# Alternating the two row halves in 64-row products, and four kinds of steps that resume a set time later

## The chip, the cores and the metric

The kernel runs on one core of one Trainium2 chip. The metric is device time in microseconds (us), from launch to the end of the core's last instruction; less is better. TensorE (PE) multiplies 128x128 weight tiles with moving operands of up to 512 columns into PSUM, which has 8 banks of 512 float32 columns here. VectorE (DVE), ScalarE (ACT) and GpSimd (POOL) do the elementwise work, and SyncE (SP) issues most DMAs.

## The reference

Two models of two layers each, on 256 tokens of width 1024, one after the other, float32. The first alternates gated MLPs with a mixer of two attentions; the second has a mixer of three branches and a gated MLP with a short convolution.

```python
x = x + 0.5 * swiglu(rms_norm(x, g1), w_gate, w_up, w_down)       # d_ff 2816
x = x + hybrid_mixer(rms_norm(x, g), ...)     # NSA, 8 heads of 64; MoBA, 8 heads of 64
x = x + 0.5 * swiglu(rms_norm(x, g2), ...)
# second model
h = rmsnorm(x, norm1_g)
p_rw, p_ret, p_sg, gates = split(h @ w_in)
# RWKV-7, 8 heads of 64, a state step for each token:
state = state * w_t + (state @ -kk_t) x (kk_t * a_t) + v_t x k_t ;  y_t = state @ r_t
# retention, 4 heads: q, k of 64, v of 128, in chunks of 128 tokens:
scores = einsum('bhnid,bhnjd->bhnij', qc, kc) * decay_in ;  inner = scores @ vc
x = x + sum(sigmoid(gates) * (branches @ w_branch)) @ w_out
x = x + conv_ffn(rmsnorm(x, norm2_g))
```

MoBA has one block at this length, so it is causal attention. The RWKV-7 recurrence is computed in two chunks of 128 tokens: products over a head's 64 features between the decayed r, kk, k and b give 128x128 matrices; a strictly triangular system is solved in blocks of 32.

## The kernel before, in words

The 256 tokens are two tiles `t` of 128 rows. All large products are done in three passes of float32r: an operand is split into a rounded part and the rest (`wh`, `wl` of a weight tile; `xh`, `xl` of the transposed activations). A weight tile of 512 KB is loaded into `raw` on SP's queue (5 buffers), ACT casts it to `wh`, DVE subtracts to `wl`, and TensorE takes it with 24 matmuls of 256 columns (banks `cf`, `pj`) or 12 of 512 (`pj`, `acc`). That stream runs from start to end.

Everything else is cut into steps. A step is what a Python generator does between two `yield`s (`norm`, `rw_keys`, `rw_products`, `rw_chain`, `group_norm`, ...). `tick` (line 295), called between the matmuls of the stream, adds steps of tasks that are due, by rank. Due times come from a cost model of the builder (`Meter`, line 130): `step` (line 272) remembers the modelled end of the last instruction off TensorE in a step, and after a bare `yield` the task is due 0.1 us after that end. The model is only a plan: it fixes the order of the instructions on each engine, and the engines then run through it in order. All instructions are issued through one wrapper, so the trace shows line 191 for each; tiles tell them apart.

Names used below:

- `norm` (531): the transposed x; then the row factor `xr` by ACT (`junk`) and POOL, and, for `wide`, a step whose product `pt<-ident,xr` spreads it over partitions for `factor`. Eight phases have it, for two `t` each.
- `rw_keys` (1468): `pn` and POOL's power give `n` (one number for a token and a head), `pr` spreads it; then `pL`, the products of all 16 heads and tiles, copied to `Ld` and masked to `Lo`. `Ld` goes out to memory and back as `Lc`.
- `rw_chain` (1634): 31 rounds on DVE (`Tt`, `T`) invert the blocks from `Lc`; the result goes out and back to `dbd` by 9 DMAs, and the substitution (`pS`) reads that.
- `rw_products` (1598): for each `t` and head, `pM` (64 rows; one product of 128 columns, one of 256), copied under a mask to `mrb` and `lm`; in the next step `pX` and `pY` multiply `lm` with v.
- `group_norm` (1727): the branch output `Y`, then transposed (`pt<-ident,Y`).
- `moba` (970): scores `sc<-kmT,qmT`; `retention` (1288): scores `rs<-qkT`.

Head pairs are stacked: rows 0 to 63 of `kr`, `bh`, `KT`, `qkT`, `kmT`, `qmT` hold the even head, rows 64 to 127 the odd one. A float32 product counts as two matmul records in the trace, one of float32r as one.

Of the kernel before, what the change touches and what calls it, by code (L numbers as in the profile page):

```python
# [17 lines left out]
P = 128  # L18
# [204 lines left out]
class Builder:  # L223
# [48 lines left out]
    def step(self, task):  # L272
        self.meter.last = self.meter.t["PE"]
        try:
            y = next(task.gen)
        except StopIteration:
            self.tasks.remove(task)
            return
        if y is None:
            task.ready = self.meter.last + 0.1  # L280
        elif callable(y):
            task.cond = y
        else:
            task.ready = self.meter.of(y) + 0.1
# [246 lines left out]
    def norm(self, t, gi, wide=False, outer=None):  # L531


        nc = self.nc
        F = "p (k f) -> p k f"
        for i in range(2):
            yield from self.have(t, i)
            pt = self.ps("pt")
            for k in range(4):
                c = slice(k * P, (k + 1) * P)  # L540
                nc.tensor.transpose(pt[:, c], self.half(t, i)[:, c], self.ident)
            k = slice(i * 4, i * 4 + 4)
            g = self.gains if outer is None else self.both
            o = gi * KD if outer is None else 0
            g = g[:, o + i * 4:o + i * 4 + 4, None].to_broadcast([P, 4, P])
            xg = self.u("xg").rearrange(F, f=P)
            nc.vector.tensor_tensor(xg, pt.rearrange(F, f=P), g, ALU.mult)
            nc.scalar.copy(self.xh[:, k, t], xg)
            yield [self.xh[:, i * 4, t]]
            nc.vector.tensor_tensor(self.xl[:, k, t], xg, self.xh[:, k, t].bitcast(F32), ALU.subtract)  # L550
            self.ready_xT[t] = i + 1
        yield
        if outer is not None:
            ro = yield from self.row_norm(t, outer)
        r = yield from self.mean_sq(t)
        if outer is not None:
            nc.gpsimd.tensor_tensor(r, r, ro, ALU.mult)
        self.rstd[t] = r
        if wide:
            yield  # L560
            if not self.factor:
                self.factor.append(self.u("factor"))
            pt = self.ps("pt")
            nc.tensor.matmul(pt[:, :P], r.to_broadcast([P, P]), self.ident, start=True, stop=True)
            nc.scalar.copy(self.factor[0][:, t * P:(t + 1) * P], pt[:, :P])
            self.factored.append(t)
# [150 lines left out]
        self.nc.scalar.copy(o, pt)  # L717
        return o.rearrange("p (k f) -> p k f", f=P)

    def attend(self, jobs, place, factor, fresh):  # L720

# [1 line left out]
        nc = self.nc  # L725
        sms, pes, ptss = {}, {}, {}
        for i in range(len(jobs) + 4):
# [24 lines left out]
            if i < len(jobs):  # L752
                t, j, units = jobs[i]
                w = P * (t + 1)
                mask = self.c("cmask")[:, 256 - w:256]
                sms[i] = []
                for score, _ in units:
                    ps = self.ps("sc")
                    score(ps, w)
                    sm = self.u("sm")  # L760
                    mn = self.small("mn", 2, 6)
                    for e in range(2):
                        c = slice(e * w, (e + 1) * w)
                        nc.vector.tensor_tensor_reduce(sm[:, c], ps[:, c], mask, op0=ALU.add, op1=ALU.min, scale=-0.125,
                                                       scalar=BIG, accum_out=mn[:, e:e + 1])
                    sms[i].append((sm, mn))
# [27 lines left out]
    def mixer1(self, l, after):  # L794
# [75 lines left out]
        def vs(e, kb, g):  # L870
            return kv1[kb][:, 384 + g * 64:448 + g * 64] if e == 0 else kv2[kb][:, 128 + g * 64:192 + g * 64]
# [25 lines left out]
        def nsa():  # L897
# [26 lines left out]

            def unit(t, h):
                g = h // 4

                def score(ps, w):
                    q = qst[t, g][:, h % 4]
                    nc.tensor.matmul(ps[:, :2 * w], q, kh[g][:, :, 0:t + 1], start=True, stop=False)  # L930
                    nc.tensor.matmul(ps[:, :2 * w], q, kl[g][:, :, 0:t + 1], start=False, stop=True)

                return score, lambda e, kb: vs(e, kb, g)

            def factor(t, j, r, sums):
                nc.vector.reciprocal(r, sums)
# [7 lines left out]
            def place(t, j, u, e):  # L944
                return out_of(t)[64 * u:64 * u + 64, j * P:(j + 1) * P]

            for y in self.attend(jobs, place, factor, False):
                yield y
                n += 1
                if n in (1, 2):  # L950
                    for z in cmp:
                        yield z
                        break
                if n == 3:
                    yield from cmp
                for t, at in ((0, 8), (1, 12)):
                    if n == at:
                        self.begin(split_oT(0, t, out[t]), 0)
# [11 lines left out]
        def moba():  # L970
# [10 lines left out]
                return out[t][64 * u:64 * u + 64, (2 * j + e) * P:(2 * j + e + 1) * P]  # L981

            def unit(t, j, u):
                def score(ps, w):
                    b = slice(64 * u, 64 * u + 64)
                    for e in range(2):
                        for kb in range(t + 1):
                            nc.tensor.matmul(ps[:, e * w + kb * P:e * w + (kb + 1) * P], qmT[t][b, 2 * j + e],
                                             kmT[kb][b, 2 * j + e], start=True, stop=True)

                return score, lambda e, kb: vm[kb][:, (4 * j + 2 * e + u) * 64:(4 * j + 2 * e + u + 1) * 64]

            def factor(t, j, r, sums):
                nc.vector.reciprocal(r, sums)

            n = 0
            for y in self.attend([(t, j, [unit(t, j, u) for u in range(2)]) for t in range(NT) for j in range(2)],
                                 place, factor, True):
                yield y
                n += 1  # L1000
                for t, at in ((0, 6), (1, 8)):
                    if n == at:
                        self.begin(split_oT(1, t, out[t]), 0)
# [284 lines left out]
    def retention(self, qk, rv, rg, done):  # L1288
# [23 lines left out]
        yield  # L1312
        for t in range(NT):
            sc = self.u("rsc")
            for par in range(2):
                b = 64 * par
                ps = self.ps("rs")
                for j in range(2):
                    nc.tensor.matmul(ps[:, j * P:(j + 1) * P], qkT[t][b:b + 64, 2 + j], qkT[t][b:b + 64, j],
                                     start=True, stop=True)  # L1320
                nc.vector.tensor_tensor(sc.rearrange("p (j r f) -> p j r f", j=2, r=2)[:, :, par],
                                        ps[:, :256].rearrange(F, f=P),
                                        self.c("rdec").rearrange("p (j r f) -> p j r f", j=2, r=2)[:, :, par], ALU.mult)
            yield
            y = self.u("yret")
# [142 lines left out]
    def rw_keys(self, l, st):  # L1468
# [16 lines left out]
        n = self.small("n2", 16, 2)  # L1485
        nc.vector.tensor_scalar_max(n, pn[:, :16], 1e-24)
        nc.gpsimd.tensor_tensor(n, n, self.mh, ALU.pow)
        yield
        for q in range(2):
            pr = self.ps("pr")  # L1490
            kk.append(self.pairs("kk"))
# [30 lines left out]
            off[t, par] = self.u("Lo").rearrange(F, f=P)  # L1522
            tt(off[t, par], pv, self.c("moff")[:, None].to_broadcast([P, 4, P]), ALU.mult)

        late = None
        for t in range(NT):
            for par in range(2):
                b = 64 * par
                pL = self.ps("pL")
                for j in range(4):  # L1530
                    mm(pL[:, j * P:(j + 1) * P], BT[j // 2][b:b + 64, j % 2, t], kr[j // 2][b:b + 64, j % 2, t, 0],
                       start=True, stop=True)
                s0 = (t * 2 + par) * 4
                pv = pL.rearrange(F, f=P)
                for blk in range(4):
                    c = slice(32 * blk, 32 * blk + 32)
                    nc.scalar.copy(Ld[c, s0:s0 + 4], pv[c, :, c])
                if late:
                    rest(*late)
                late = t, par, pv  # L1540
                yield
        rest(*late)
        for blk in range(4):
            nc.sync.dma_start(sysd[blk].rearrange("y s t -> s y t"), Ld[32 * blk:32 * blk + 32])
        Lc = self.up.tile([P, 32, 32], F32, tag="kr", name="Lc")
# [52 lines left out]
    def rw_products(self, l, st):  # L1598
# [13 lines left out]
        for t in range(NT):  # L1612
            m = mrb[t]
            pX, pY = self.ps("pX", "pq"), self.ps("pY", "pq")
            for h in range(8):
                b, q, e = 64 * (h % 2), h // 4, h // 2 % 2
                pM = self.ps("pM")
                mm(pM[:, 0:P], BT[q][b:b + 64, e, t], kr[q][b:b + 64, e, t, 1], start=True, stop=True)
                mm(pM[:, P:3 * P], KT[q][b:b + 64, e, t], kr[q][b:b + 64, e, t].rearrange("p z f -> p (z f)"), start=True, stop=True)
                lm = st["lm"][h % 4]  # L1620
                nc.vector.copy_predicated(m[:, h], mk[:, 0:P], pM[:, 0:P])
                nc.vector.copy_predicated(lm, mk[:, P:3 * P], pM[:, P:3 * P])
                yield
                c = slice(h * 64, (h + 1) * 64)
                self.narrow(pX[:, c], lm[:, 0:P], v[t][:, c])
                self.narrow(pY[:, c], lm[:, P:2 * P], v[t][:, c])
            X.append(self.u("X"))
            Y.append(self.u("Y"))
            nc.scalar.copy(X[t], pX)
# [97 lines left out]
    def group_norm(self, lnx, y, v, bonus, g, done):  # L1727
# [18 lines left out]
        tt(y, y, lnx[0], ALU.mult)  # L1746
        tt(y, y, bv, ALU.add)
        tt(y, y, g, ALU.mult)
        yield
        yield from done(y)  # L1750


# [95 lines left out]
```

## Time and profile before

| | |
|---|---|
| three runs, median | 2075.59 us (2074.72 to 2077.48) |
| profiled execution | 2073.28 us, its span 2071.3 us |
| TensorE matmul busy | 2013.7 us, 97% |
| DVE, ACT, POOL busy | 67%, 50%, 7% |
| DMA | 343.98 MB, 166 GB/s on average |
| granted TensorE clock, mean | 0.990 |

A busy TensorE is the time in which at least one matmul record is open. Records overlap, since matmuls are pipelined, so the distance from one start to the next is the time that one costs. The granted clock is 1.00 at 2.4 GHz and 0.50 at 1.2 GHz.

### The profile page before, as it was taken

Reading aid. Unit: us, or ns where it says so; the run is one execution under the profiler, and the core shown is the slowest. Engines: PE = TensorE matmul, PEld = TensorE weight load, DVE = VectorE, ACT = ScalarE, POOL = GpSimd, SP = SyncE. Lnnn points to the kernel's source line nnn. Section 1 sums busy time; section 2 is a strip of 40 time slices with the busy share of each in tenths; the row PEclk is TensorE's granted clock in tenths of the full one; section 3 lists DMA queues with packets and bytes.
Section 4 is the critical chain, followed back from the end, with each engine's and each line's share of the span. In section 5 each row is a group of like instructions: output and inputs, shape, how many; then the busy total and the mean of one; then the engine's idle time right before and its main releaser. Section 6 shows DMA issues by size and latency. Waiting matters only on the chain. (4 is left out here: it accounts for less than half of the span.)

```text
span 2071.3 us, 33930 instructions
## 1 busy us (share of the span) xinstructions
PE 2013.7 (97%) x13548; PEld 1776.8 (86%) x13548; DVE 1394.7 (67%) x2101; ACT 1043.6 (50%) x1605; POOL 149.8 (7%) x168
## 2 busy tenths in 40 slices
PE   8999999999999999999999999999999999999998
PEld 8998878998999887799887777889988877789997
DVE  6665666664666467666567957669955886667983
ACT  5444675443444366544455434456636444446652
POOL 0000000000000010000021031210001003110000
PEclk9999999999999999999999999999999999999999
DMA  9655623656655562356653434555664453465562
GB/s 315 195 181 152 213 83 113 198 177 194 218 180 185 157 214 92 122 174 193 186 175 114 147 112 136 180 162 177 191 200 134 133 153 98 153 192 176 177 194 97
DMA packets 246733, 343.98 MB, mean 166 GB/s; under 512 B 22064, under 2 KB 182192, under 8 KB 246448
## 3 DMA queue, kind: packets, MB, share of 16 engines
q1 hardware_dynamic: 244224, 340.20, 52.8%
q8 instruction: 106, 1.74, 0.4%
q10 hardware_dynamic: 2352, 1.63, 0.3%
q14 instruction: 51, 0.42, 0.1%
HBM read 339.68 MB, written 2.10 MB: 165 GB/s over the span
## 5 line engine op out<-in xcount | busy, mean ns | idle before, releaser
L191 DVE TENSOR_TENSOR wl<-raw,wh 128x1024 fp32r<-128x1024 f32 (+1 forms) x614 | 750.8, 1236 | 323.9 <-ACT wh L191 323.0
L191 ACT CAST wh<-raw 128x1024 fp32r<-128x1024 f32 (+1 forms) x614 | 639.3, 1046 | 585.9 <-PE cf L191 179.6
L191 PE MATMUL cf<-xh,wh 128*128 128x256 f32 x2112 | 524.7, 285 | 2.4 <-ACT wh L191 2.4
L191 PE MATMUL cf<-xl,wh 128*128 128x256 f32 x2112 | 523.0, 285 | 0.0
L191 PEld LDWEIGHTS cf<-xh,wh 128*128 128x128 f32 x2112 | 409.3, 194 | 3.0 <-ACT wh L191 2.8
L191 PEld LDWEIGHTS cf<-xl,wh 128*128 128x128 f32 x2112 | 409.2, 194 | 0.2
L191 PE MATMUL cf<-xh,wl 128*128 128x256 f32 x2112 | 300.3, 285 | 0.0
L191 PEld LDWEIGHTS cf<-xh,wl 128*128 128x128 f32 x2112 | 275.3, 194 | 0.0
L191 PE MATMUL pj<-wh,xh 128*128 128x512 f32 (+1 forms) x544 | 223.0, 410 | 4.5 <-DVE gate L191 2.0
L191 PE MATMUL pj<-wl,xh 128*128 128x512 f32 (+1 forms) x544 | 211.1, 388 | 0.0
L191 PE MATMUL pj<-wh,xl 128*128 128x512 f32 (+1 forms) x544 | 210.4, 387 | 0.0
L191 PE MATMUL acc<-wh,h 128*128 128x512 f32 x528 | 207.0, 392 | 0.0
L191 PE MATMUL acc<-wh,hl 128*128 128x512 f32 x528 | 205.6, 389 | 0.0
L191 PE MATMUL acc<-wl,h 128*128 128x512 f32 x528 | 205.5, 389 | 0.0
L191 PEld LDWEIGHTS pj<-wh,xh 128*128 128x128 f32 x544 | 102.8, 189 | 36.7 <-issue 9.9
L191 DVE TENSOR_TENSOR up<-cf,factor 128x512 f32<-128x512 f32 x132 | 90.6, 688 | 56.3 <-PE cf L191 56.2
L191 PEld LDWEIGHTS pj<-wh,xl 128*128 128x128 f32 x544 | 102.8, 189 | 21.4
L191 PEld LDWEIGHTS pj<-wl,xh 128*128 128x128 f32 x544 | 103.1, 189 | 16.9 <-DVE wl L191 0.9
L191 PEld LDWEIGHTS acc<-wh,hl 128*128 128x128 f32 x528 | 99.1, 188 | 20.9
L191 PEld LDWEIGHTS acc<-wh,h 128*128 128x128 f32 x528 | 99.2, 188 | 20.0
L191 PEld LDWEIGHTS acc<-wl,h 128*128 128x128 f32 x528 | 99.2, 188 | 19.9
L191 POOL TENSOR_SCALAR xv<-ss 128x1 f32<-128x1 f32 x24 | 20.2, 840 | 1142.6 <-ACT junk L191 1142.6
(314 smaller groups left out, 2489.6 us busy)
## 6 DMA issues: line engine op xcount, KB each, us to landing
raw<-w_in SPq DMA_DIRECT2D x156, 512.0 KB, 4.3
raw<-w_ffn_gate SPq DMA_DIRECT2D x88, 512.0 KB, 4.4
raw<-w_ffn_up SPq DMA_DIRECT2D x88, 512.0 KB, 4.8
raw<-w_ffn_down SPq DMA_DIRECT2D x88, 512.0 KB, 4.2
raw<-ffn_w_up SPq DMA_DIRECT2D x88, 512.0 KB, 4.7
raw<-ffn_w_down SPq DMA_DIRECT2D x44, 512.0 KB, 4.5
raw<-w_out SPq DMA_DIRECT2D x32, 512.0 KB, 3.7
raw<-w_branch SPq DMA_DIRECT2D x24, 512.0 KB, 4.5
```

What stands on the lines that cost most here:

```text
L191: return f(*args, **kw)
```

## The change

A `yield` of a number makes a task due that many modelled microseconds after the step's last instruction off TensorE. Four steps use it: the spreading of `xr` (5.0), of `n` (3.0), the products `pX`, `pY` (0.8), and the transposing of `Y` (2.0). The products over 64 rows of two heads, of the even and of the odd rows, are written alternately, into two PSUM banks that are claimed first. So `rw_products` takes two heads in a step and `pL` both row halves of a token tile. In `attend` a job's two score banks are claimed before its products; the NSA scores, which have 128 rows, keep their order.

```diff
@@ step
+        elif isinstance(y, float):
+            task.ready = self.meter.last + y
@@ norm
-            yield
+            yield 5.0
@@ attend
-                for score, _ in units:
-                    ps = self.ps("sc")
-                    score(ps, w)
+                banks = [self.ps("sc") for _ in units]
+                scores([x for x, _ in units], banks, w)
+                for ps in banks:
@@ moba
-                    for e in range(2):
-                        for kb in range(t + 1):
+            def scores(keys, banks, w):
+                for e in range(2):
+                    for kb in range(keys[0][0] + 1):
+                        for (t, j, b), ps in zip(keys, banks):
                             nc.tensor.matmul(ps[:, e * w + kb * P:e * w + (kb + 1) * P], qmT[t][b, 2 * j + e],
                                              kmT[kb][b, 2 * j + e], start=True, stop=True)
@@ retention
+            rs = [self.ps("rs") for par in range(2)]
+            for j in range(2):
+                for par in range(2):
+                    b = slice(64 * par, 64 * par + 64)
+                    nc.tensor.matmul(rs[par][:, j * P:(j + 1) * P], qkT[t][b, 2 + j], qkT[t][b, j], start=True, stop=True)
...
@@ rw_keys
-        yield
+        yield 3.0
...
-            for par in range(2):
-                b = 64 * par
-                pL = self.ps("pL")
-                for j in range(4):
...
+            pL = [self.ps("pL") for par in range(2)]
+            for j in range(4):
+                for par in range(2):
+                    b = slice(64 * par, 64 * par + 64)
+                    mm(pL[par][:, j * P:(j + 1) * P], BT[j // 2][b, j % 2, t], kr[j // 2][b, j % 2, t, 0], start=True,
+                       stop=True)
...
+            for par in range(2):
+                rest(t, par, pv[par])
+            yield
@@ rw_products
-            for h in range(8):
...
-                nc.vector.copy_predicated(m[:, h], mk[:, 0:P], pM[:, 0:P])
-                nc.vector.copy_predicated(lm, mk[:, P:3 * P], pM[:, P:3 * P])
-                yield
+            for j in range(4):
+                q, e = j // 2, j % 2
+                pM = [self.ps("pM") for z in range(2)]
+                bs = [slice(64 * z, 64 * z + 64) for z in range(2)]
+                for z, b in enumerate(bs):
+                    mm(pM[z][:, 0:P], BT[q][b, e, t], kr[q][b, e, t, 1], start=True, stop=True)
+                for z, b in enumerate(bs):
+                    mm(pM[z][:, P:3 * P], KT[q][b, e, t], kr[q][b, e, t].rearrange("p z f -> p (z f)"), start=True, stop=True)
+                lms = [st["lm"][(2 * j + z) % 4] for z in range(2)]
+                for z in range(2):
+                    nc.vector.copy_predicated(lms[z], mk[:, P:3 * P], pM[z][:, P:3 * P])
+                for z in range(2):
+                    nc.vector.copy_predicated(m[:, 2 * j + z], mk[:, 0:P], pM[z][:, 0:P])
+                yield 0.8
+                for z in range(2):
...
@@ group_norm
-        yield
+        yield 2.0
```

On TensorE, in the second phase with a wide norm (the first model's second MLP), the spreading of `xr` for the first token tile stands here before, with buffer numbers (`cf` is a bank pair of the stream, `wh` a weight tile):

```order
L191 MATMUL cf_3634<-xh_3476,wh_3541 128x256
L191 MATMUL cf_3634<-xl_3477,wh_3541 128x256
L191 MATMUL cf_3634<-xh_3476,wh_3541 128x256
L191 MATMUL cf_3634<-xl_3477,wh_3541 128x256
L191 MATMUL pt_3702<-ident_76,xr_3658 128x128
L191 MATMUL cf_3634<-xh_3476,wh_3541 128x256
L191 MATMUL cf_3634<-xl_3477,wh_3541 128x256
```

and here now:

```order
L191 MATMUL cf_3634<-xh_3450,wh_3625 128x256
L191 MATMUL cf_3634<-xl_3451,wh_3625 128x256
L191 MATMUL cf_3634<-xh_3450,wh_3625 128x256
L191 MATMUL cf_3634<-xl_3451,wh_3625 128x256
L191 MATMUL pt_3776<-ident_76,xr_3658 128x128
L191 MATMUL cf_3634<-xh_3450,wh_3625 128x256
L191 MATMUL cf_3634<-xl_3451,wh_3625 128x256
```

It moved from the second weight tile of the phase to the fourth: two tiles, 48 matmuls of the stream, later.

On TensorE in the mixer of the second model's first layer, the first heads' `pM`, `pX` and `pY` among the projections `pj` stand so before:

```order
L191 MATMUL pX<-vt,lm 64x64 x2
L191 MATMUL pY<-vt,lm 64x64 x2
L191 MATMUL pM<-kr,bh 128x128
L191 MATMUL pM<-kr,KT 128x256
L191 MATMUL pj_11705<-wh,xh 128x512
L191 MATMUL pj_11705<-wl,xh 128x512
L191 MATMUL pj_11705<-wh,xl 128x512
```

and so now:

```order
L191 MATMUL pX<-vt,lm 64x64 x2
L191 MATMUL pY<-vt,lm 64x64 x2
L191 MATMUL pX<-vt,lm 64x64 x2
L191 MATMUL pY<-vt,lm 64x64 x2
L191 MATMUL pM<-kr,bh 128x128 x2
L191 MATMUL pM<-kr,KT 128x256 x2
L191 MATMUL pj_11698<-wh,xh 128x512
L191 MATMUL pj_11698<-wl,xh 128x512
L191 MATMUL pj_11698<-wh,xl 128x512
```

Two heads share a step, and the stream is left 8 times instead of 16 in a layer. Between the layer's first `pM` and the `pX` of its seventh head 159 `pj` stand before; 153 stand between the first `pM` and the `pX` of the eighth pair, the last, now.

On DVE in the same layer, in the middle of the 31 rounds (`Tt`, `T`), before:

```order
L191 TENSOR_REDUCE T<-Tt 128x16
L191 TENSOR_TENSOR wl<-raw,wh 128x1024
L191 COPY_PREDICATED mrb<-cst,pM 128x128
L191 COPY_PREDICATED lm<-cst,pM 128x256
L191 TENSOR_TENSOR wl<-raw,wh 128x1024
L191 TENSOR_TENSOR Tt<-T,Lc 128x272
```

and now:

```order
L191 TENSOR_REDUCE T<-Tt 128x16
L191 TENSOR_TENSOR wl<-raw,wh 128x1024
L191 COPY_PREDICATED lm<-cst,pM 128x256 x2
L191 COPY_PREDICATED mrb<-cst,pM 128x128 x2
L191 TENSOR_TENSOR Tt<-T,Lc 128x272
```

Between the first and the last round stand the copies of 14 heads instead of 6 in this layer (12 instead of 6 in the other), and 10 `wl` instead of 11 (9 instead of 11).

## Rows read from the trace of the kernel before

**Rows 1.** The page's first part: busy time, share of the span and instructions.
```profile
PE 2013.7 (97%) x13548; PEld 1776.8 (86%) x13548; DVE 1394.7 (67%) x2101; ACT 1043.6 (50%) x1605; POOL 149.8 (7%) x168
```

**Rows 2.** Waits of TensorE: waiter, releaser: us in total, times, longest us.
```profile
PE pt L191 <- POOL xr L191: 19.1, 9, 3.2
PE pr L191 <- POOL n L191: 4.9, 2, 2.8
...
PE pX L191 <- DVE lm L191: 3.6, 7, 1.3
PE pt L191 <- DVE Y L191: 3.4, 2, 1.7
```

**Rows 3.** Timeline, 341.5 to 350 us: start, length, engine, instruction [idle before <-releaser].
```profile
344.54 1.39 POOL L191 TENSOR_TENSOR xr<-xv,mh 128x1 f32<-128x1 f32 x1
...
345.98 0.64 PE L191 MATMUL pt<-ident,xr 128*128 128x128 f32 x2 [3.24 <-POOL xr L191]
```

**Rows 4.** Windows: stretch, length, busy (count) by engine, granted clock, DMA share, GB/s.
```profile
346.20:349.60 3.40, 3.40 (x17) 3.40 (x17) 0.44 (x1) 2.54 (x6) 0.86 (x2) 0.50 0.99 338
360.00:363.40 3.40, 3.40 (x31) 3.40 (x30) 3.40 (x4) 1.36 (x2) 0.00 (x0) 1.00 0.27 65
...
1092.70:1097.10 4.40, 4.38 (x27) 4.01 (x27) 1.66 (x4) 1.02 (x4) 0.20 (x1) 0.50 0.00 0
...
1374.87:1380.40 5.53, 5.53 (x26) 5.53 (x27) 1.88 (x2) 2.54 (x6) 2.66 (x4) 0.50 0.86 295
1568.20:1571.50 3.30, 3.30 (x17) 3.30 (x17) 2.01 (x3) 2.81 (x6) 0.00 (x0) 0.50 1.02 349
1602.30:1605.70 3.40, 3.40 (x25) 3.01 (x23) 0.67 (x2) 0.00 (x0) 0.00 (x0) 0.50 0.00 0
```

**Rows 5.** Timeline of PE around one `pL` block, one row half alone.
```profile
1103.38 1.16 PE L191 MATMUL pL<-kr,bh 64*128 64x128 f32 x8
1104.46 0.39 PE L191 MATMUL pj<-xh,wh 128*128 128x256 f32 x1
```

**Rows 6.** Timeline of PE: MoBA's scores, both row halves, four and eight records each.
```profile
306.32 0.72 PE L191 MATMUL sc<-kmT,qmT 64*128 64x128 f32 x8
...
309.40 1.71 PE L191 MATMUL sc<-kmT,qmT 64*128 64x128 f32 x16
```

**Rows 7.** Timeline of PE around one step of the products.
```profile
1133.84 0.40 PE L191 MATMUL pj<-wh,xl 128*128 128x512 f32 x1
1134.17 0.34 PE L191 MATMUL pX<-vt,lm 128*64 128x64 f32 x4
...
1134.55 0.49 PE L191 MATMUL pM<-kr,bh 64*128 64x128 f32 x2
...
1135.40 0.50 PE L191 MATMUL pj<-wh,xh 128*128 128x512 f32 x1
1135.74 0.40 PE L191 MATMUL pj<-wl,xh 128*128 128x512 f32 x1
```

**Rows 8.** Windows, the 31 rounds of the first layer.
```profile
1125.80:1178.60 52.80, 52.05 (x272) 39.63 (x272) 50.14 (x90) 21.60 (x25) 0.00 (x0) 1.00 0.41 130
```

**Rows 9.** Groups of DVE in that stretch: count, busy us, mean ns, idle before.
```profile
L191 DVE TENSOR_TENSOR Tt<-T,Lc 128x32 f32<-128x32 f32 (+30 forms) x31 | 20.5, 661 | 0.8
L191 DVE TENSOR_TENSOR wl<-raw,wh 128x1024 fp32r<-128x1024 f32 x13 | 16.2, 1254 | 0.0
L191 DVE TENSOR_REDUCE T<-Tt 128x16 f32<-128x32 f32 (+30 forms) x31 | 13.6, 439 | 1.1
L191 DVE COPY_PREDICATED lm<-cst,pM 128x256 f32<-128x256 uint32 x6 | 2.6, 440 | 0.0
L191 DVE COPY_PREDICATED mrb<-cst,pM 128x128 f32<-128x128 uint32 x6 | 1.8, 298 | 0.8 <-PE pM L191 0.8
```

**Rows 10.** Group of PE, from the first `pX` at 1134.16 us to 1180.30 us.
```profile
L191 PE MATMUL pj<-wh,xl 128*128 128x512 f32 x52 | 20.3, 390 | 0.0
```

**Rows 11.** SP's queue, 1176 to 1200 us.
```profile
1191.31 5.14 SPq L191 DMA_DIRECT2D dbd<-invd  x8
```

More of the change, by code (lines that the diff above doesn't have):

```diff
@@ L718, in transpose4, with attend @@
         return o.rearrange("p (k f) -> p k f", f=P)
-    def attend(self, jobs, place, factor, fresh):
+    def attend(self, jobs, scores, place, factor, fresh):
         nc = self.nc
@@ L926, in unit @@
                 g = h // 4
-                def score(ps, w):
+                return (t, h), lambda e, kb: vs(e, kb, g)
+            def scores(keys, banks, w):
+                for (t, h), ps in zip(keys, banks):
+                    g = h // 4
                     q = qst[t, g][:, h % 4]
@@ L931, in score @@
                     nc.tensor.matmul(ps[:, :2 * w], q, kl[g][:, :, 0:t + 1], start=False, stop=True)
-                return score, lambda e, kb: vs(e, kb, g)
             def factor(t, j, r, sums):
@@ L945, in place @@
                 return out_of(t)[64 * u:64 * u + 64, j * P:(j + 1) * P]
-            for y in self.attend(jobs, place, factor, False):
+            for y in self.attend(jobs, scores, place, factor, False):
                 yield y
@@ L983, in unit, with scores @@
             def unit(t, j, u):
-                def score(ps, w):
-                    b = slice(64 * u, 64 * u + 64)
-                    for e in range(2):
-                        for kb in range(t + 1):
+                return (t, j, slice(64 * u, 64 * u + 64)), lambda e, kb: vm[kb][:, (4 * j + 2 * e + u) * 64:(4 * j + 2 * e + u + 1) * 64]
+            def scores(keys, banks, w):
+                for e in range(2):
+                    for kb in range(keys[0][0] + 1):
+                        for (t, j, b), ps in zip(keys, banks):
                             nc.tensor.matmul(ps[:, e * w + kb * P:e * w + (kb + 1) * P], qmT[t][b, 2 * j + e],
                                              kmT[kb][b, 2 * j + e], start=True, stop=True)
-                return score, lambda e, kb: vm[kb][:, (4 * j + 2 * e + u) * 64:(4 * j + 2 * e + u + 1) * 64]
             def factor(t, j, r, sums):
@@ L997, in moba @@
             for y in self.attend([(t, j, [unit(t, j, u) for u in range(2)]) for t in range(NT) for j in range(2)],
-                                 place, factor, True):
+                                 scores, place, factor, True):
                 yield y
@@ L1314, in retention @@
             sc = self.u("rsc")
-            for par in range(2):
-                b = 64 * par
[L1317 to L1320, printed above, removed]
+            rs = [self.ps("rs") for par in range(2)]
[3 more added lines that the diff above has]
+                    nc.tensor.matmul(rs[par][:, j * P:(j + 1) * P], qkT[t][b, 2 + j], qkT[t][b, j], start=True, stop=True)
+            for par in range(2):
                 nc.vector.tensor_tensor(sc.rearrange("p (j r f) -> p j r f", j=2, r=2)[:, :, par],
-                                        ps[:, :256].rearrange(F, f=P),
+                                        rs[par][:, :256].rearrange(F, f=P),
                                         self.c("rdec").rearrange("p (j r f) -> p j r f", j=2, r=2)[:, :, par], ALU.mult)
@@ L1523, in rest @@
             tt(off[t, par], pv, self.c("moff")[:, None].to_broadcast([P, 4, P]), ALU.mult)
-        late = None
         for t in range(NT):
-            for par in range(2):
-                b = 64 * par
-                pL = self.ps("pL")
-                for j in range(4):
-                    mm(pL[:, j * P:(j + 1) * P], BT[j // 2][b:b + 64, j % 2, t], kr[j // 2][b:b + 64, j % 2, t, 0],
-                       start=True, stop=True)
+            pL = [self.ps("pL") for par in range(2)]
[4 more added lines that the diff above has]
+                       stop=True)
+            pv = [x.rearrange(F, f=P) for x in pL]
+            for par in range(2):
                 s0 = (t * 2 + par) * 4
-                pv = pL.rearrange(F, f=P)
                 for blk in range(4):
                     c = slice(32 * blk, 32 * blk + 32)
[L1537 to L1540, printed above, removed]
-                yield
-        rest(*late)
+                    nc.scalar.copy(Ld[c, s0:s0 + 4], pv[par][c, :, c])
+            for par in range(2):
+                rest(t, par, pv[par])
+            yield
         for blk in range(4):
@@ L1614, in rw_products @@
             pX, pY = self.ps("pX", "pq"), self.ps("pY", "pq")
-            for h in range(8):
[L1616 to L1620, printed above, removed]
-                nc.vector.copy_predicated(m[:, h], mk[:, 0:P], pM[:, 0:P])
-                nc.vector.copy_predicated(lm, mk[:, P:3 * P], pM[:, P:3 * P])
-                yield
-                c = slice(h * 64, (h + 1) * 64)
-                self.narrow(pX[:, c], lm[:, 0:P], v[t][:, c])
-                self.narrow(pY[:, c], lm[:, P:2 * P], v[t][:, c])
+            for j in range(4):
[13 more added lines that the diff above has]
+                for z in range(2):
+                    h = 2 * j + z
+                    c = slice(h * 64, (h + 1) * 64)
+                    self.narrow(pX[:, c], lms[z][:, 0:P], v[t][:, c])
+                    self.narrow(pY[:, c], lms[z][:, P:2 * P], v[t][:, c])
             X.append(self.u("X"))
@@ L1748, in group_norm @@
         tt(y, y, g, ALU.mult)
-        yield
+        yield 2.0
         yield from done(y)
```

## The prediction, made blind

> **What bounds the kernel now.** I began with busy time: TensorE is open for work in 97% of the span, DVE in 67% [rows 1]. So time is won only where TensorE waits, runs at a lower clock, or needs fewer issue slots. TensorE's waits come second: the four yields touch the largest of them. `pt` waits for `xr` 9 times, 19.1 us in all, `pr` for `n` 4.9, `pt` for `Y` 3.4; `pX` for `lm` 3.6 [rows 2]. The timeline shows the first as a single hole: POOL finishes `xr` at 345.93, and TensorE has been idle for 3.24 us [rows 3]. The stream's matmuls behind that `pt` are free to run, but the queue is in order. Third come windows with the granted clock. Behind the hole 17 matmuls take 3.40 us at 0.50; 14 us later 31 take 3.40 at 1.00, 0.11 each [rows 4]. Last I read the timeline around the 64-row products, and DVE in the one stretch where it is nearly full: 50.14 of 52.80 us while the 31 rounds run [rows 8].
>
> **Spreading `xr`, 5.0.** The product moves behind 48 more matmuls, 48 x 0.11 = 5.3 us, where the longest wait is 3.2: I take all 19.1. The half-clock stretches follow the holes; at 346.20 the 17 matmuls would need 1.9 us instead of 3.40, at 1374.87 the 26 need 2.9 instead of 5.53 [rows 4]. There are five such (346, 541, 872, 1375, 1568): 4 x 1.5 + 2.6 = 8.6, of which I take 7, since other idle time may still lower the clock in places. Together 26.1. What pays for the delay is the eviction of the first gate products, which need `factor` and so come 5 us later. A group of these is 96 matmuls (four weight tiles), 10.6 us, and the banks hold four groups; that covers it. If it didn't, each of the eight phases would wait up to 5.
>
> **`n`, 3.0.** `pr` moves behind 33 matmuls of 256 columns in the first layer, 3.6 us, and 20 in the second, 2.2, against waits of 2.8 and 2.1 (4.9 less the longest) [rows 2]; so the margin is 0.8 and 0.1. All 4.9, then. The half-clock stretches behind them, 4.40 and 3.40 us [rows 4], would halve: 3.9, I take 3.5. Together 8.4, with 5 as the lower bound. Queued behind `pr` are the steps that make `kr` and `bh`, so the chain starts some 3 us later (below).
>
> **`Y`, 2.0.** The waits are 1.7 each [rows 2], and the move is 1.9: 3.4.
>
> **The pairs.** One step of the products: from the start of `pX` at 1134.17 to the first `pj` behind it at 1135.40 is 1.23 us [rows 7]. Its neighbours are long too: 0.33 from the last `pj` before to `pX`, 0.34 from the first `pj` behind to the next. An undisturbed `pj` is 0.24 (below), so entering and leaving cost 0.1 each, and a step 1.43. Two heads now cost 2.86. Do two row halves run beside each other? MoBA's scores say so: 8 records of both halves take 0.72 us [rows 6], 8 of one half 1.16 [rows 5]. So a pair's `pM` cost what one head's cost, only `pX` and `pY` are added (from 1134.17 to 1134.55, 0.38 with the entry; 0.25 without): 1.23 + 0.25 + 0.2 = 1.68. It saves 1.18 for a pair, and 16 pairs 18.9. A `pL` block takes 1103.38 to 1104.46, 1.08 [rows 5], and 0.2 for the way in and out; 4 of the 8 blocks disappear beside their partner: 5.1. Scores of the second tile: 16 records in 1.71 are only partly side by side; at 0.11 a record and the 0.39 by which 1.16 exceeds seven of them, eight slots would be 1.16: 0.55 each, four of them, 2.2. The first tile's are side by side already: 0. Retention's `rs` I put at 0.25 for each of 4 (0 to 0.43, the gain that 0.72 shows against 1.16): 1.0. Sum 27.2.
>
> The Trainium skill ("TensorE: Matmul & The Clock Gate", Part 3, "The mechanism") says that matmuls keep program order in start and end. By it the first tile's scores, written head after head, would run one after another and alternating would save 4 x 0.44, 1.8 us more. The trace doesn't agree, since 0.72 is already there [rows 6].
>
> **What is late next: DVE in the rounds.** Between first and last round now stand 14 heads' copies instead of 6 and one `wl` less. A head's two copies are 0.44 + 0.30 = 0.74 [rows 9]; but the five groups add up to 54.7 in 50.14 of busy time, so they overlap and a head is 0.68: 8 x 0.68 = 5.4 more, 1.25 x 0.92 = 1.15 less. The stretch becomes 52.8 + 5.4 - 1.15 = 57.0 us. TensorE in it: 52.05 busy, less the steps of six heads, 6 x 1.43, plus seven pairs, 7 x 1.68, less the 12 `pj` of the missing `wl`, 12 x 0.24: 52.4. (The 0.24: the stretch of 46.1 us in rows 10 less six steps, by three times 52 `pj` [rows 10].) So DVE is 4.7 behind, and TensorE will stand at `pX` for `lm`. I take 5 a layer, with what DVE then hands on late to retention's transposes; bounds 0 (the `wl` made ahead hold the gap) and 8 (one us for each pair). The old waits on `lm`, 3.6 [rows 2], are in that and go. Net -6.4.
>
> Behind the rounds the inverse goes out and back: the last round ends at 1178.6 [rows 8], `dbd` has landed at 1191.31 + 5.14 = 1196.45 [rows 11], 17.9 us later. Since all products are then done earlier, `pS` stands close to that, about 18 us behind the rounds by its place. I take 0, with 4 a layer as the bound.
>
> **Sum.** 26.1 + 8.4 + 3.4 + 27.2 - 6.4 = 58.7. From the profiled execution, 2073.28 us, that is 2014.6; the median of the runs is 2.3 above it, so 2017.
>
> **The rivals.**
> 1. DVE takes over through all the products, in the rounds and around them, and what the `pM` pairs save, 18.9, comes back as waits on `lm`: 2036. For it speaks that only 2.7 us of DVE are free in the rounds [rows 8]; against it that copies outside of the rounds meet a DVE that is a third idle. The Trainium skill ("TensorEngine Tiling (Array Packing)", "PSUM Bottleneck") states it as a rule: packing speeds up TensorE and leaves the eviction of PSUM as it was, which can then bound. The trace agrees that the two are close in this stretch alone.
> 2. The yields don't do what they say. The planner's times are modelled, and a wait may form again at the new place, or the half clock with another cause. Half of 26.1 + 8.4 + 3.4 = 37.9 lost gives 2036, all of it 2055. For it: the margin of 0.1 at the second `n`. Against: 5.3 us of stream for a wait of 3.2.
> 3. The halves don't overlap in these products: 27.2 lost, 2044. Only if the two 0.72 blocks [rows 6] are an exception.
> 4. Slower: changing the row half with each product empties the array. The price would be what entering and leaving a step costs, 0.2, per record of an alternating block; there are 128 in `pM`, 64 in `pL`, 96 in the scores and 32 in `rs`, 320 in all: 64 us plus the lost 27.2, 2108. It decides once a change costs over 0.1, since then 320 x 0.1 eats the 31.5 of the rest. The 0.72 speaks against it, where both halves were in flight.
> 5. Waits that return and halves that don't overlap, both: 37.9 + 27.2 = 65 against 58.7, and no DVE excess: about 2076, no change.
>
> **Chances.** Forecast 0.69 (its own range 2003 to 2031), rival 1 0.13, rival 2 0.08 for half and 0.02 for all, rival 3 0.03, rival 4 0.03, rival 5 0.02. Low end: no wait on DVE (10 less), all 8.6 of the clock, `rs` at 0.43: about 2004, and 2003. The forecast's high end: 8 a layer for DVE (+6) and 4 a layer for `dbd` (+8). To 2042 the range takes in rival 1 and half of rival 2. Under 0.2%, 4 us, the measurement can't tell the kernels apart; rival 5 lies within it, rival 4 above, with 0.01 for what I don't see: faster 0.94, same 0.02, slower 0.04.
>
> **What would show it.** Right: no wait of TensorE on `xr`, `n` or `Y` of over 0.5 us; the half-clock windows at 346 and 1375 gone; a pair of `pM` as eight records in the 0.85 us that four take now; `pX` waiting on `lm` some 4 to 5 us a layer, all within the rounds, and DVE over 95% busy there. Wrong: an eviction of `cf` or a `cf` matmul that waits for DVE at the start of the phases (the cover), `pS` waiting on `dbd` (the round trip), `pM` records of both halves at the old pitch (rival 3 or 4). If the rounds take over 60 us, rival 1 holds.

## The result, and the profile after

The changed kernel takes 2038.67 us (median of 4 runs, 2036.28 to 2043.77) against 2076.53 for the kernel before beside it: 0.9822 of it, 95% interval 0.9801 to 0.9842, 38 us less. Measured again on another chip it was 0.9832 (0.9817 to 0.9847). The forecast was 2017, 59 less. The result lies inside the stated range only because that range was drawn up to 2042 to take in rivals 1 and 2; the forecast's own range ended at 2031.

The page's first part of the changed kernel: as in [rows 1], nearly all of the span is TensorE.

```profile
PE 1986.1 (97%) x13548; PEld 1757.4 (86%) x13548; DVE 1391.0 (68%) x2101; ACT 1042.0 (51%) x1605; POOL 156.3 (8%) x168
```

Waits of TensorE in it, to be laid beside [rows 2]: `xr` and `n` have gone from the list. `lm` has grown from 3.6 to 9.3; `up` was 1.5 before and `S` wasn't there; one of the two waits on `Y` is left. (`up`, `gate`, `sv` and `qk` are what is copied out of the banks `pj`; `S` is the state that the recurrence hands from the first token tile to the second; `X` and `sa` belong to its substitution.)

```profile
PE pX L191 <- DVE lm L191: 9.3, 10, 1.8
PE pj L191 <- DVE up L191: 5.4, 2, 2.9
...
PE pX L191 <- DVE S L191: 2.9, 1, 2.9
...
PE pt L191 <- DVE Y L191: 1.7, 1, 1.7
```

Timeline at the place of [rows 3]: `xr` is ready at 347.47, and TensorE takes it at 349.90 without a pause.

```profile
346.08 1.39 POOL L191 TENSOR_TENSOR xr<-xv,mh 128x1 f32<-128x1 f32 x1
...
349.90 0.38 PE L191 MATMUL pt<-ident,xr 128*128 128x128 f32 x2
```

Timeline of PE, the products. A pair's step runs from 1131.75 to 1133.22, 1.47 us; one head's took 1.23 [rows 7]. Eight `pM` records of a pair take the place of four. MoBA's 16 records take 1.16 where they took 1.71 [rows 6], and 16 of `pL` take the 1.16 that 8 did [rows 5].

```profile
312.33 1.16 PE L191 MATMUL sc<-kmT,qmT 64*128 64x128 f32 x16
...
1092.69 1.16 PE L191 MATMUL pL<-kr,bh 64*128 64x128 f32 x16
...
1131.75 0.34 PE L191 MATMUL pX<-vt,lm 128*64 128x64 f32 x4
...
1132.37 0.49 PE L191 MATMUL pM<-kr,bh 64*128 64x128 f32 x4
1132.69 0.60 PE L191 MATMUL pM<-kr,KT 64*128 64x256 f32 x4
1133.22 0.50 PE L191 MATMUL pj<-wh,xh 128*128 128x512 f32 x1
```

Windows: the stream's matmuls that ran at half clock at 346 before stand from 344.1 on here and run at full clock, 31 in 3.40 us where it was 17 [rows 4]; then the rounds of the first layer [rows 8].

```profile
344.00:347.40 3.40, 3.40 (x31) 3.40 (x30) 3.40 (x5) 3.25 (x7) 3.15 (x2) 1.00 0.97 314
...
1111.90:1172.40 60.50, 55.40 (x354) 41.22 (x352) 54.00 (x102) 21.03 (x25) 2.04 (x2) 0.94 0.36 115
```

**Where the time went.** This profile is of the longest of its four runs (2043.77). I therefore take the sums from the second profile of the same kernel (`after_again`, 2037.94), 35.3 below the profiled execution of before. Each stretch below begins and ends at the same matmul of the weight stream in both traces; "half clock" is half the length of the stretches granted at 0.50.

| stretch | forecast | measured |
|---|---|---|
| starts of the six phases where TensorE stood at `xr` | -26.1 | -25.7 |
| first model's start and attention (scores -2.2) | -2.2 | +1.4 |
| the two mixers of the second model | -30.4 | -11.8 |
| of that: waits over 0.1 us | -1.9 | +7.2 |
| of that: half clock | -3.5 | +1.7 |
| of that: the rest, by the forecast slots on TensorE | -25.0 | -20.7 |

The -26.1 is for all nine waits on `xr`. The six starts hold 17.6 of their 19.1 us, so 24.6 of the forecast is theirs. Of the +1.4 in the first model 1.1 stand in its first phase, where TensorE now waits 1.4 us for `wh` and no longer 0.8 for `xr`; the attention's stretches are 0.1 longer. The end of the kernel, about 1 us longer, makes up the rest.

So `xr` came about as worked out and most of the slots did, and the mixers gave nearly half of the slots back in waits and clock. Timeline of PE and windows of that second profile show places where half clock follows a wait: the wait on `up` is followed by 3.40 us at 0.50, that on `lm` at 1151.27 and that on `Y` too. It isn't so at each wait: behind the 2.31 us on `S` at 1706.6 the clock stays at 1.00, and between the stretch from 1105.20 and the next, from 1115.40, there is no wait of over 0.4 us. The first two windows below are the rounds of the two layers.

```profile
1105.04 0.69 PE L191 MATMUL pj<-wh,xh 128*128 128x512 f32 x1 [2.44 <-DVE up L191]
...
1151.27 0.34 PE L191 MATMUL pX<-vt,lm 128*64 128x64 f32 x4 [1.60 <-DVE lm L191]
...
1230.11 0.41 PE L191 MATMUL pt<-ident,Y 128*128 128x128 f32 x2 [1.74 <-DVE Y L191]
```

```profile
1111.80:1169.70 57.90, 54.99 (x358) 41.17 (x355) 53.52 (x103) 21.25 (x25) 1.22 (x1) 0.94 0.34 109
1605.60:1659.50 53.90, 50.65 (x329) 38.27 (x328) 51.54 (x97) 20.71 (x25) 1.96 (x2) 0.97 0.34 109
1105.20:1108.60 3.40, 3.40 (x9) 2.66 (x10) 2.84 (x4) 1.38 (x3) 0.00 (x0) 0.50 0.75 196
...
1153.00:1156.40 3.40, 3.40 (x9) 2.62 (x10) 3.26 (x5) 0.00 (x0) 0.00 (x0) 0.50 0.42 134
1231.50:1234.90 3.40, 3.23 (x23) 2.58 (x23) 2.42 (x4) 1.31 (x3) 0.00 (x0) 0.50 0.15 20
```

The wait on `up` itself comes down DVE's queue. Timeline of DVE in the changed kernel: four `Lo` stand one behind the other and wait for ACT's copies `Ld`, 1.55 + 0.39 + 0.94 + 0.43 = 3.3 us. Before, each `Lo` stood one step late, and the steps held one row half. From there DVE is busy until the eviction `up` at 1105.62, for which TensorE waits until 1106.36. That the four waits make the one on `up` is argued from this order; no run here frees DVE of them.

```profile
1094.97 0.69 DVE L191 TENSOR_TENSOR Lo<-pL,cst 128x512 f32<-128x512 f32 x1 [1.55 <-ACT Ld L191]
1096.06 0.69 DVE L191 TENSOR_TENSOR Lo<-pL,cst 128x512 f32<-128x512 f32 x1 [0.39 <-ACT Ld L191]
1097.70 0.69 DVE L191 TENSOR_TENSOR Lo<-pL,cst 128x512 f32<-128x512 f32 x1 [0.94 <-ACT Ld L191]
1098.82 0.69 DVE L191 TENSOR_TENSOR Lo<-pL,cst 128x512 f32<-128x512 f32 x1 [0.43 <-ACT Ld L191]
...
1105.62 0.68 DVE L191 TENSOR_TENSOR up<-pj,factor 128x512 f32<-128x512 f32 x1
```

### The profile page after: what moved, and what is told of

Same layout as the page of the kernel before. It is cut to its first block, busy times and chain, and to the rows that moved or that the text cites. A ratio compares the mean times of both kernels' runs of the same rounds, so it can differ in the third digit from the quotient of the medians.

```text
span 2042.0 us, 33943 instructions
## 1 busy us (share of the span) xinstructions
PE 1986.1 (97%) x13548; PEld 1757.4 (86%) x13548; DVE 1391.0 (68%) x2101; ACT 1042.0 (51%) x1605; POOL 156.3 (8%) x168
## 5 line engine op out<-in xcount | busy, mean ns | idle before, releaser
L191 PEld LDWEIGHTS acc<-wh,hl 128*128 128x128 f32 x528 | 99.1, 188 | 20.7
```

Source lines behind the costliest of these rows:

```text
L191: return f(*args, **kw)
```

## The experiments

Each ratio is to the kernel before, run beside it, with its 95% interval.

**1. The yield of 5.0 alone.** `xr_only`:

```diff
+        elif isinstance(y, float):
+            task.ready = self.meter.last + y
...
-            yield
+            yield 5.0
```

> The kernel before with the yield of 5.0 alone, all else as it was. My term for it: 19.1 us of waits and about 7 of half-clock stretches, 26 less, so about 2050. In the changed kernel's trace the six phases with this product start behind it 24.8 us earlier in sum. If that holds alone, 2050 to 2052. Rival, that the later eviction gives it back or that half-clock stretches form elsewhere: under 15 less, 2061 or more.

2058.14 us, 0.9928 (0.9915 to 0.9940): 15.5 less, between the two. The phase starts gave 25.6, as in the changed kernel. But the second layer's mixer is 9 longer: new waits stand there, one of 4.9 us on `sa`, which POOL cleared late, since it had stood 9.9 us for the DMA of `ws`. That the later start shifted these steps against the stream is likely, but not shown.

```profile
PE pS L191 <- ACT sa L191: 5.4, 2, 4.9
```

**2. All four yields, no pairs.** `yields_only` adds to that:

```diff
-        yield
+        yield 3.0
...
-                yield
+                yield 0.8
...
-        yield
+        yield 2.0
```

> The kernel before with all four yields (5.0, 3.0, 0.8, 2.0), heads one after another as before, and the masked copies Lo of pL one step late as before. Forecast of the prediction for these: 38 less, 2038, with no pj that waits for an eviction (up) behind n. Theory now: the wait of pj for up, 5.4 us in the changed kernel, comes from the paired pL step, where Lo no longer stands one step late; here it is absent, and the time is 2038 to 2043. Rival: the wait for up comes from n being later itself, since the steps behind pr come late on DVE; then up is waited for here too, 4 us or more in both layers, and the time is 2046 or more.

2046.33, 0.9873 (0.9858 to 0.9888): 27 less instead of 38. `up` is waited for 1.9 us, not 5.4, so the later `n` alone doesn't make that wait; but `yret` has one of 5.3, again one that the list of before doesn't hold. The time lies at the rival's, for another cause than the rival's.

```profile
PE pt L191 <- DVE yret L191: 5.3, 1, 5.3
...
PE pj L191 <- DVE up L191: 1.9, 2, 1.2
```

**3. The pairs alone.** `pairs_only` is the changed kernel with

```diff
-            yield 5.0
+            yield
...
-        yield 3.0
+        yield
...
-                yield 0.8
+                yield
...
-        yield 2.0
+        yield
```

> The changed kernel with the four yields bare: the pairs alone. The prediction's terms: 27.2 less for the slots, 6.4 back for DVE in the rounds, so about 2055. Theory now: the rounds cost what was forecast, but the paired pL step holds DVE at Lo (waiting for ACT's Ld), some 4 to 5 us with its half clock, so 12 to 16 less, 2060 to 2064. If the halves gave nothing, 2076 or more.

2068.30, 0.9981 (0.9971 to 0.9991): 4 to 5 less, where the slots are worth 20. In the mixers the waits grew by 11.6 (5.3 and 6.3), and ahead of the end 41 us run at half clock, against 37.5 before. The waits of TensorE show where it went:

```profile
PE pX L191 <- DVE lm L191: 10.3, 11, 1.8
PE pS L191 <- ACT sa L191: 5.4, 2, 3.3
...
PE pj L191 <- DVE up L191: 4.4, 2, 2.7
```

**4. `Lo` one step late again.** `late_lo`, and the same file once more as `late_again`:

```diff
                     nc.scalar.copy(Ld[c, s0:s0 + 4], pv[par][c, :, c])
+            yield
             for par in range(2):
                 rest(t, par, pv[par])
-            yield
```

> The changed kernel, in which the two Lo of a token tile stand behind the yield of the pL step again, one step late, as the kernel before had it. Theory: DVE no longer stands at Lo for ACT's Ld (3.3 us in the first layer), the eviction up behind it comes in time, and pj's wait for up, 5.4 us, goes, with part of the half-clock stretches behind it: 5 to 8 less than the changed kernel's 2038.7, 2031 to 2034. Rival: n's step itself made DVE late; up is still waited for, and the time is within 2 us of the changed kernel.

2030.54, 0.9795 (0.9781 to 0.9809). Faster as expected, but not for the reason: `up` is waited for 5.9 us. DVE still waits 1.57 and 0.39 at the first two `Lo`, and now stands 2.0 at `k` for ACT's `c`, which comes behind the `Ld`. So it waits for ACT as long as before, 4.0 instead of 3.3 us, and this run doesn't tell whether those waits make the one on `up`.

> The changed kernel once more, beside the version with Lo one step late on one chip: is that version faster, and does the profile of the changed kernel hold? Its first profile is of its longest run (2043.8). I expect a median of 2036 to 2040, the same waits by place (up 5.4, lm 9.3), and half-clock stretches elsewhere or fewer. If the profile was typical, five such stretches ahead of the end again, 24 us.

> The version with Lo one step late, a second time. If its 8 us are real: 2029 to 2032 beside the changed kernel's 2036 to 2040. Rival: chips and runs differ by that much, and the two lie within 3 us of each other.

The changed kernel 2038.43, this version 2034.18, 0.9810 (0.9793 to 0.9827); the runs (2037.94 to 2039.05, 2031.18 to 2036.31) don't overlap, though the intervals of the two ratios do. With `late_lo` the version has come out faster twice, by 4 to 8 us. The half clock carries it, not the waits: in the mixers 7 us run at half clock in either profile, against 20 in `after_again`; the 13 fewer are worth half of that, some 7 us. The waits in the mixers add up to as much as before, 27 and 29 against 27.5 (those over 0.1 us, as in the table): `Y` is gone, but `S` has grown from 2.3 to 4.8 and `lm` by 3. Why the clock falls less often with as much waiting stays open. Its waits, in `late_again`:

```profile
PE pX L191 <- DVE lm L191: 9.9, 11, 1.8
PE pj L191 <- DVE up L191: 5.9, 2, 3.0
...
PE pX L191 <- DVE S L191: 4.8, 2, 2.5
```

**5. `Ld` cut in two again.** `ld_split`, on the version with the late `Lo`:

```diff
...
+                if late:
+                    rest(*late)
+                late = t, par, pv[par]
+                yield
-            yield
-            for par in range(2):
-                rest(t, par, pv[par])
...
```

> The version with Lo one step late (2030.5 us), in which ACT's copies Ld and the Lo of the two row halves stand in steps of their own again (the products of both halves still alternate). Theory now: pj waits for up, 3 us in each layer, because the paired step gives ACT 8 copies Ld in one piece (2.1 us, twice), behind which its c, v and DVE's k, KT, kr and up come late; cut in two, the wait falls to the 1.2 and 0.7 of the kernel with the yields alone, 4 us less and some half clock: 2024 to 2028. Rival: up is late for another reason, since the pairs bring the products forward; then up is still waited for, 2.5 us or more in both layers, and the time is 2029 to 2033.

2034.21, 0.9807 (0.9794 to 0.9821), no gain. `up` fell by 2.1, so ACT's eight copies in one piece are at most a part of it; that they are one isn't shown, since `in_turn` below keeps them in one piece and has 3.7. There, in the first layer, ACT's `c` stands ahead of its `v`, and DVE waits 1.30 for it instead of 2.00 in `late_again`. `Y` and `gate` are waited for again.

```profile
PE pj L191 <- DVE up L191: 3.8, 2, 2.3
PE pj L191 <- DVE gate L191: 2.6, 2, 2.0
...
PE pt L191 <- DVE Y L191: 1.7, 1, 1.7
```

**6. `pX`, `pY` 3.0 later.** `lag3`, on the same version:

```diff
-                yield 0.8
+                yield 3.0
```

> The version with Lo one step late, in which pX and pY resume 3.0 instead of 0.8 later. Theory: in the rounds DVE is the bound, and the 10.3 us in which pX waits for lm only change their place: pj waits for wl or up instead, or the rounds end later; within 3 us of 2030.5. Rival: the waits on lm are only a matter of where pX stands in the queue; they go, 8 us less, 2020 to 2024.

2031.06, 0.9791 (0.9776 to 0.9806): nothing, as the theory had it. Half of the wait on `lm` is gone, and `qk` and others have taken its place; the rounds take 55.0 and 53.3 us with DVE 53.2 and 51.3 busy.

```profile
PE pX L191 <- DVE lm L191: 5.3, 4, 2.1
...
PE pt L191 <- DVE qk L191: 3.7, 2, 2.1
```

```profile
1109.00:1164.00 55.00, 53.42 (x335) 41.68 (x334) 53.15 (x98) 24.08 (x29) 1.20 (x1) 0.99 0.37 121
1597.20:1650.50 53.30, 51.34 (x308) 39.86 (x306) 51.33 (x92) 24.36 (x29) 1.20 (x1) 0.99 0.36 118
```

**7. The copies `mrb` left out.** `no_mrb`, on the same version:

```diff
-                for z in range(2):
-                    nc.vector.copy_predicated(m[:, 2 * j + z], mk[:, 0:P], pM[z][:, 0:P])
```

> The version with Lo one step late without the copies mrb (so the intra-chunk products of the bonus path lack their matrix): DVE has 14 and 12 times 0.25 us less in the rounds, 3.5 and 3.0. Theory: DVE is the bound there, so the waits of pX on lm, 10.3, fall by about 6 and the time by 6 to 8, to 2023 to 2026. Rival: pX waits for the order (two wl stand ahead of the pair's lm), not for DVE's load; then lm is waited for as before, 8 or more, and the time is within 3 us of 2030.5.

2025.57, 0.9771 (0.9756 to 0.9786), 8.6 below `late_again` beside it and 5.0 below the first run of that version. The time did what the theory said, the waits did what the rival said:

```profile
PE pX L191 <- DVE lm L191: 11.4, 11, 2.0
```

The windows of the rounds settle it, here and in `late_again`: they are shorter by 2.7 and 2.0 us, DVE's busy time by 2.7 and 2.0, and DVE is busy 96 to 97% of them in all four.

```profile
1109.60:1161.10 51.50, 46.42 (x301) 35.10 (x300) 49.65 (x86) 20.78 (x26) 1.27 (x1) 1.00 0.34 105
1596.50:1647.40 50.90, 46.46 (x317) 34.80 (x315) 49.02 (x86) 19.86 (x24) 1.26 (x1) 1.00 0.33 105
```

```profile
1111.80:1166.00 54.20, 50.51 (x321) 38.89 (x320) 52.35 (x97) 22.94 (x27) 1.28 (x1) 1.00 0.35 112
1602.40:1655.30 52.90, 48.78 (x327) 37.20 (x326) 51.04 (x98) 20.34 (x24) 1.16 (x1) 1.00 0.31 101
```

So DVE sets the length of the rounds in this version, one to one; the total of the waits on `lm` doesn't measure it. What TensorE gained shows at other tiles: its waits in the two mixers add up to 23 us instead of 27 and 29, and the 4.8 on `S` are gone.

**8. `n` with its bare yield.** `n_bare`, on the same version:

```diff
-        yield 3.0
+        yield
```

> The version with Lo one step late, in which n's step has its bare yield again. My term for n: 4.9 of wait and 3.5 of half clock, so 8 us more, 2037 to 2040, with pr waiting for n about 2.5 us in each layer. Rival, that a removed wait is made up for at the next place (pj at up, 5.9 now): the wait on n returns, those on up go, and the time is within 3 us of 2030.5.

2042.14, 0.9842 (0.9829 to 0.9856). The ratio is 0.0032 to 0.0047 above the two runs of its base, 7 to 10 us, the size of the term of 8.4. The parts are not the term's. Part of the rival is true: as `n` is waited for again, 4.1, `up` falls from 5.9 to 1.9. What is left is half clock, 20 us of it in the mixers against 7 in either profile of the base, and waits on `KT`, `Y` and `gate`.

```profile
PE pr L191 <- POOL n L191: 4.1, 2, 2.3
...
PE pt L191 <- DVE KT L191: 2.3, 1, 2.3
PE pj L191 <- DVE up L191: 1.9, 1, 1.9
```

**9. `Y` with its bare yield.** `y_bare`, on the same version:

```diff
-        yield 2.0
+        yield
```

> The version with Lo one step late with a bare yield ahead of the transposing of Y. My term: 1.7 in each layer, so 3 to 4 more, 2033.5 to 2035. Rival: the delay only trades this wait for others behind it (X, gate), within 2 us.

2037.23 (2034.40 to 2040.10), 0.9826 (0.9807 to 0.9845), 3.0 above `late_again` beside it. That is the size of the term of 3.4, but the intervals overlap; it is not shown.

**10. The row halves one after the other.** `in_turn`, on the same version; `pL`, the scores and `rs` likewise:

```diff
                 for z, b in enumerate(bs):
                     mm(pM[z][:, 0:P], BT[q][b, e, t], kr[q][b, e, t, 1], start=True, stop=True)
-                for z, b in enumerate(bs):
                     mm(pM[z][:, P:3 * P], KT[q][b, e, t], kr[q][b, e, t].rearrange("p z f -> p (z f)"), start=True, stop=True)
```

> The version with Lo one step late, with the steps as they are but the products of the two row halves written one half after the other (pM, pL, MoBA's scores, rs), into the same banks. If TensorE takes up products of the other half out of turn over a few places, as the first scores did before (8 records in 0.72 us), pM's cost nearly nothing more (4 records each) and pL (8 and 8) and the second tile's scores lose as 1.71 stands to 1.16: 4 x 0.55 each, 4 to 6 us more, 2034 to 2037. If products run strictly in the order written, the pairs' saving is gone but for the ways in and out: 16 x 0.85 + 4 x 0.9 + 8 x 0.4 = 20 us more, 2050. A third case, that the alternation is what matters little: within 2 us.

2031.73, 0.9793 (0.9780 to 0.9807): nothing. A pair's `pM` takes what it takes when alternating, 0.86 us from 1119.57 to the next `pj` (0.85 in the changed kernel), and only `pL` and the scores are back at 1.71. Timeline of PE:

```profile
1091.35 1.71 PE L191 MATMUL pL<-kr,bh 64*128 64x128 f32 x16
...
1119.57 0.50 PE L191 MATMUL pM<-kr,bh 64*128 64x128 f32 x4
1119.90 0.61 PE L191 MATMUL pM<-kr,KT 64*128 64x256 f32 x4
1120.43 0.50 PE L191 MATMUL pj<-wh,xh 128*128 128x512 f32 x1
```

So what pays in `pM` is that two heads stand in one step; in which order they are written there doesn't matter. Of the 4 x 0.55 in `pL` and as much in the scores nothing reaches the total that could be told. Waits are shorter here: `pv` waits 3.9 for `pts` instead of 4.4, so that the attention's stretches are as long as in the other versions, and `up` is down to this:

```profile
PE pj L191 <- DVE up L191: 3.7, 2, 2.4
```

## Why the prediction was right in kind, and a third of its gain did not come

1. **`xr`: right.** 25.7 at the six starts, for which 24.6 of the 26.1 were meant, and the cover held: no `cf` matmul waits for an eviction at the phase starts.
2. **`n`: the wait went, but the half clock didn't, and here the working failed.** That the yield is worth 7 to 10 where the term was 8.4 is partly luck, since the parts are others (experiment 8). The sentence "Queued behind `pr` are the steps that make `kr` and `bh`, so the chain starts some 3 us later" named what is queued behind and priced it at nothing. Behind the paired `pL` step on DVE stands `up`, and TensorE waits for it 5.4 us, 3.9 more than before, and half clock follows there in `after_again`. Both edits have a part in it: `up` is 1.9 with the yields alone, 4.4 with the pairs alone, and, with `Lo` late, 5.9 with the pairs and all yields and 1.9 with a bare `n`. DVE's waits for ACT, 3.3 us ahead of `up`, may be a part of it, but experiment 4 only moved them, and with ACT's `Ld` cut in two `up` is still waited for 3.8 (experiment 5); the cause stays open.
3. **`Y`: half.** The first layer keeps its 1.7 in the changed kernel. A move of 1.9 for a wait of 1.7 leaves a margin of 0.2; the prediction has both numbers and took all of the 3.4. What used up the margin isn't shown.
4. **The pairs: the step was sized rightly; the alternating is not what makes it.** A step of 1.47 and 0.2 around it is 1.67, against 1.68. The remainder in the mixers that was meant for slots fell by 20.7 of 25.0; where the other 4.3 are isn't shown. That halves run beside each other was read rightly from the 0.72; that they must alternate for it was not said by that row, whose products were written head after head, and experiment 10 shows that a pair's `pM` needn't. The Trainium skill ("TensorE: Matmul & The Clock Gate", Part 3, "The mechanism") says that matmuls keep program order in start and end. The trace doesn't agree, here for the second time: by it `in_turn` would have been some 20 us slower, an estimate by the working quoted there, and it was not slower.
5. **The scores: 1.16 each, and not in the total.** The attention's stretches came out 0.1 longer, not 2.2 shorter: TensorE's waits in them have grown, among them those of `pv` for `pts` by 0.5. The working had no wait behind the scores.
6. **DVE in the rounds: right in length, in part by chance.** 57.0 us were forecast for the first layer; they take 57.9 in `after_again` and 60.5 in the first profile. But DVE is busy for 53.5 and 54.0 of them, 92% and 89%, not the over 95% that was named as the sign: it stands there for `pM` (1.6 and 0.6 us in `after_again`) while TensorE is at half clock. In the second layer it is 51.5 of 53.9, 96%. New waits on `lm` of 10 were forecast, all within the rounds; 6.8 and 9.3 are found, 4.8 and 6.5 of them within. Experiment 7 shows DVE as the bound in the version with the late `Lo`, whose rounds run at full clock. The first profile's 60.5, with 6.8 us at half clock in it, passes the 60 that I had set as the mark of rival 1, the second's doesn't. DVE as the bound holds, then, in the rounds; rival 1's time, 2036, was nearly met, but by another way: its 18.9 us of waits on `lm` didn't come.
7. **The round trip by `dbd`: right**, 0: `pS` never waits for it in the changed kernel.
8. **The sum lacked a term.** I gave each removed wait its half clock back, and to the waits that I forecast I gave none, nor any allowance for those at places not looked at (`S`, `sv`, `X`). Of the 18.6 us that the mixers fell short, 9.1 are such waits, 5.2 is half clock and 4.3 is the remainder that was meant for slots.

A part of the spread is chance of the order: `xr_only` and `yields_only` each carry one wait of 5 us that no other version has, and moving `Lo` by one step gives 4 to 8 us, mostly in half clock at other places.

## What to carry to other kernels

When an engine that is 97% busy is freed of a wait, price the next wait with what may follow it, the half clock included: here 7 us of new waits in two mixers took the clock's gain with them. The sum of waits on a tile isn't the price of the engine that makes it; compare its busy time with the length of the stretch, and take a piece of its work away. And two 64-row products in opposite row halves need only to be near each other in the queue: four records and four didn't have to alternate here.

## What the runs showed of the hardware that I had not expected

TensorE takes up a product of the other row half ahead of its turn, but not from far. At 0.39 us and 0.11 for each record behind the first, 0.72 us [rows 6] is four slots: four records and four of the other half, written one half after the other, run fully side by side. Eight and eight written so take 1.71, 13 slots, and alternating 1.16, eight. So three slots of 16 were saved there. The starts of the single records in `in_turn`'s `pL` say the same: from 1091.35 on they come one by one, and a second row of them begins at 1091.91, beside the fifth (1091.90). So alternating matters at eight records of a half, and at four, as in a head's `pM`, it doesn't; what lies between was not run. The prediction's sentence that the queue is in order holds for the hole of [rows 3], where ready matmuls stood behind a `pt` that waited, but not between the row halves.
